# The S5 mixing stages of a four-layer trunk: fixed TensorE order, float32 in-projection in layer 0, u's round trip on the sync queue, decay tables ahead of the data

## The chip, the cores and the metric

The kernel runs on one core of a Trainium2 chip. The metric is the device time of one execution in microseconds (us), lower is better. The kernel before takes 1125.99 us, the median of three runs (1124.99 to 1126.99). A profile of one more execution shows what each engine did: TensorE (PE, and PEld for its weight loads), VectorE (DVE), ScalarE (ACT), GpSimd (POOL) and the sync engine (SP), which here only issues DMAs.

## What is computed

A trunk of four layers over 512 tokens of width 1024. Layers 0 and 3 mix with S5, layer 1 with HGRN2, layer 2 with sliding-window attention. Each layer adds `RMSNorm(branch(RMSNorm(h)))` to `h`. Only the S5 branch is touched by the change:

```python
def s5_branch(h, w_in, lam_re, lam_im, log_dt, b_re, b_im, c_re, c_im, d_skip, w_glu, b_glu, w_out):
    proj = h @ w_in                                   # 1024 -> 2048
    u, z = proj[..., :1024], proj[..., 1024:]
    uf = u.reshape(bsz, seq, 64, 16)                  # 64 groups of 16 channels
    ...                                               # a = exp(lambda dt), per group 64 complex states
    xr = jnp.einsum('blgh,gph->blgp', uf, bbr)
    xi = jnp.einsum('blgh,gph->blgp', uf, bbi)
    _, _, sr, si = lax.associative_scan(_complex_scan_combine, (a_r, a_i, xr, xi), axis=1)
    y = jnp.einsum('ghp,blgp->blgh', c_re, sr) - jnp.einsum('ghp,blgp->blgh', c_im, si)
    y = y.reshape(bsz, seq, 1024) + d_skip * u
    y = jax.nn.gelu(y)
    y = y * jax.nn.sigmoid(y @ w_glu + b_glu)
    return (y * jax.nn.silu(z)) @ w_out
```

## The kernel before

**Order of the work.** The program is written as straight code. A list scheduler decides the order of each engine's instructions from the code order and its own estimates; a buffer pool with a fixed number of buffers per tag decides what must wait for what. Once the order is fixed, each engine runs its instructions strictly in that order, and so do the two queues that issue DMAs, SP and ACT: a DMA that waits holds back everything behind it on its queue.

**Projections.** A float32 product is made of three matmuls in a reduced float32 format (fp32r): `whi·xh + whi·xl + wlo·xh`, for each of 8 slices k of the contraction, so 24 matmuls of 512 columns for one block of 128 outputs (`ws`, L146). ACT rounds a raw weight piece `wraw` to `whi` (L112), DVE subtracts to get `wlo` (L113); the normed input is split likewise into `xh` (ACT, L210) and `xl` (DVE, L211). The in-projection of an S5 layer has 16 blocks: 8 of u, 8 of z; it reads 16 weight pieces of 512 KB. The first 4 blocks are made in column pieces of 256 and 128 while the norm of the layer is still being computed (`first_blocks`).

**The S5 stage.** u's 8 blocks go through 8 rounds b = 0 to 7.
- `s5_tables`, once a layer: powers of the decay, tiles `ap`, `eb`, `ea`, many small DVE instructions; it stands behind the layer's norm statistics.
- `s5_rot`, once for two rounds: the scan's rotation table `rot` from `ea` and `eb` (DVE; products `rt` on POOL), copied by DMA to tile `rotf`.
- `s5_block_tables(b)`: parameters `prm` by DMA (one buffer), `q` (DVE, POOL `q12b`), the filter `vt = ap·q - ...` (DVE L483 and L485, POOL product `t` L484), its transposes and taps on PE (`kps`, `ktp`, `tps`, then `v` and `toep`), and `w` (DVE L514, POOL `t2w` L515, then L516 on DVE or, for odd b, on POOL).
- `s5_u(b)`: ACT copies the block to `ut`, a DMA writes it to DRAM (`ub`), another reads it back transposed as `u`; both are issued from the ACT queue.
- `s5_core(b)`: `xps = v·u` on PE (L537); ACT swaps halves (`xsw`); DVE rotates (`xa` L544, `xsw` L545, `xa` L546), scans (`r` L548); ACT swaps (`rsw` L550, L551); DVE rotates back (`r` L552, `rsw` L553, `spre` L555); PE makes `yps` from `toep·u` (L566) and `w·spre` (L568); ACT applies gelu (`ysb` L572). After each odd b, PE transposes two rounds of `ysb` (`ytp` L580) into `y`.

The gated output (`y @ w_glu`, written "glu" below) follows when all of `y` is there. The remaining 12 in-projection blocks are written in the code between the rounds and behind them, and the scheduler spreads their matmuls over the stage.

Of the kernel before, what the change touches and what calls it, by code (L numbers as in the profile page):

```python
# [9 lines left out]
F32 = mybir.dt.float32  # L10
# [6 lines left out]
P = 128  # L17
# [32 lines left out]
class Trunk:  # L50
# [30 lines left out]
    def w_load(self, i):  # L81
        if i >= len(self.wseq) or i in self.wraw or i in self.wcv:
            return
        name, j, c = self.wseq[i]
        shape, pieces = self.w_form(name)
        self.wraw[i] = []
        for v in range(pieces):
            raw = self.wpool.tile(shape, F32, tag="wraw", name="wraw", bufs=3)
            self.nc.sync.dma_start(out=raw, in_=self.a[name][j, c, v])
            self.wraw[i].append(raw)  # L90

    def w_conv(self, i):
        if i >= len(self.wseq) or i in self.wcv:
            return
# [7 lines left out]
        for raw in raws:  # L102
# [90 lines left out]
    def norm_xt(self, L, tbs):  # L193
# [7 lines left out]
        for k2 in range(KB // per):  # L201
# [5 lines left out]
            for kk in range(per):  # L207
# [3 lines left out]
                nc.vector.scalar_tensor_tensor(out=xl[:, k, c], in0=ps[:, kk, :], scalar=g, in1=xh[:, k, c].bitcast(F32), op0=ALU.mult, op1=ALU.subtract)  # L211
# [123 lines left out]
    def s5_tables(self, j):  # L335
# [73 lines left out]

        self.sp, self.tp, self.cp = [], [], []  # L410
# [13 lines left out]
    def s5_rot(self, pr):  # L424
# [23 lines left out]
        out = []  # L448
        for i in range(2):
            f = s.tile([P, 2, 512], F32, tag=f"rot{i}", name="rotf", bufs=1)  # L450
            src = rot[64 * i:64 * i + 64]
            nc.sync.dma_start(out=f[0:64], in_=src)
            nc.sync.dma_start(out=f[64:128], in_=src)
            out.append(f)
        return out

    def s5_open(self, L):

        self.tabcm = self.tc.tile_pool(name="tab", bufs=1, side="right", reuse_waits="tile")
        self.tab = self.tabcm.__enter__()  # L460
        self.s5_tables(L // 3)

    def s5_block_tables(self, j, b):
        nc, a, s = self.nc, self.a, self.scr
# [3 lines left out]
        nc.scalar.dma_start(out=prm, in_=a["s5_bc"][j, b])  # L468
# [26 lines left out]
        ktp = self.psum.tile([P, 2, 4, 32], F32, tag="ca", name="ktp", bufs=2)
        for i in range(2):
            nc.tensor.transpose(ktp[:, i].rearrange("p g h -> p (g h)"), kt[:, i, :], self.ident)
        dmx = self.tab.tile([P, 8, 16], F32, tag="dmx", name="dmx", bufs=1)
        nc.gpsimd.tensor_tensor(out=dmx, in0=bc(t["dm"][:, gs].unsqueeze(2), [P, 8, 16]), in1=bc(self.cst[:, CO_EYE16:CO_EYE16 + 16].unsqueeze(1), [P, 8, 16]), op=ALU.mult)
        ksb = self.tab.tile([P, 2, 4, 16], F32, tag="ksb", name="ksb", bufs=2)  # L500
        nc.vector.tensor_tensor(out=ksb, in0=ktp[:, :, :, 0:16], in1=dmx.rearrange("p (a g) h -> p a g h", a=2), op=ALU.add)
        toep = self.tp[b % 2]
        for jj in range(8):
            n = (jj + 1) * 16
            nc.sync.dma_start(out=toep[128 - n:128, jj, :, :], in_=ksb[0:n].rearrange("p a g h -> p (a g) h"))
        for hh in range(2):
# [3 lines left out]
            nc.scalar.activation(out=v[:, 4 * hh:4 * hh + 4, :], in_=tps, func=AF.Copy)  # L510

        w = s.tile(shp, F32, tag="w", name="w", bufs=2)
        t2 = self.tab.tile(shp, F32, tag="t2", name="t2w", bufs=1)
        nc.vector.tensor_tensor(out=w, in0=bc(t["ap"][:, 0, gs, 1:9].unsqueeze(3), shp), in1=bc(c1[:, :, 0:16].unsqueeze(2), shp), op=ALU.mult)  # L514
        nc.gpsimd.tensor_tensor(out=t2, in0=bc(t["ap"][:, 1, gs, 1:9].unsqueeze(3), shp), in1=bc(s2.unsqueeze(2), shp), op=ALU.mult)  # L515
        (nc.gpsimd if b % 2 else nc.vector).tensor_tensor(out=w, in0=w, in1=t2, op=ALU.subtract)  # L516
        return dict(v=v, w=w.rearrange("p g j h -> p g (j h)"), toep=toep, sp=self.sp[b % 2])

    def s5_u(self, b, ps):
# [5 lines left out]
        nc.scalar.dma_start(out=ub.rearrange("j f c -> f j c"), in_=ut)  # L525
# [684 lines left out]
```

## Time and profile before

| | |
|---|---|
| median of three runs | 1125.99 us (1124.99 to 1126.99) |
| the profiled execution, its own time | 1127.56 us |
| its span in the trace | 1125.8 us |
| mean granted TensorE clock over the span | 0.968 of full speed |
| PE busy | 1039.3 us, 92% |
| DVE busy | 783.4 us, 70% |
| ACT busy | 516.8 us, 46% |
| POOL busy | 233.2 us, 21% |
| layer 0's S5 stage, up to the dense glu matmuls | 0 to about 203 us |
| layer 3's S5 stage, up to the dense glu matmuls | about 834 to 1033 us |

The span is the trace's time from the first to the last instruction; 1.76 us of the execution's own time lie outside of it. The busy shares are means over four layers with different limits, so a stage is read from its own stretch, not from this table.

### The profile page before, as it was taken

The page shows a single profiled execution, that of the slowest core. Times are in us where ns is not written, and L with a number is a line of the kernel's source. Part 1 is how long each engine was busy: PE and PEld are TensorE (multiplying, and loading weights), DVE is VectorE, ACT ScalarE, POOL GpSimd, SP SyncE. Part 2 cuts the span into 40 slices and gives each one's busy share as a digit, 9 for nine tenths or more (in the row PEclk, how much of TensorE's full clock was granted, in tenths as well). Part 3 has the DMA queues.
Part 4 walks back from the last instruction along what each step waited for, and adds up shares of the span by engine and source line. Part 5 has one row for each costly group of instructions (what it writes and reads, how often), then busy time and mean ns, then how long its engine had stood idle before and what let it go on. Part 6 is the DMA issues. An engine that isn't in the chain of part 4 may idle for free.

```text
span 1125.8 us, 16828 instructions
## 1 busy us (share of the span) xinstructions
PE 1039.3 (92%) x6384; PEld 863.8 (77%) x6384; DVE 783.4 (70%) x1442; ACT 516.8 (46%) x939; POOL 233.2 (21%) x218
## 2 busy tenths in 40 slices
PE   5987898999999999999999989999998888778997
PEld 5866676878899898989888966666688676667885
DVE  6979998675566475656656455566569799995752
ACT  5444444754332324142344344888545254446540
POOL 2165553210200000000001121100011546550200
PEclk9989989999999999999999999999999899998999
DMA  7455425333130212222123443112134644434221
GB/s 244 136 143 141 102 86 128 131 120 114 53 111 22 94 39 83 69 75 76 36 79 102 108 116 100 38 53 80 57 128 126 168 107 139 115 91 140 95 91 56
DMA packets 60320, 112.32 MB, mean 100 GB/s; under 512 B 23632, under 2 KB 33488, under 8 KB 59856
## 3 DMA queue, kind: packets, MB, share of 16 engines
q1 hardware_dynamic: 34272, 87.58, 25.5%
q10 hardware_dynamic: 25968, 23.68, 7.2%
q8 instruction: 50, 0.82, 0.3%
q14 instruction: 30, 0.25, 0.1%
HBM read 87.11 MB, written 8.39 MB: 85 GB/s over the span
## 4 chain that ended last, share of the span: by engine, by line
PE 59%; DVE 23%; issue 6%; DMA 4%; ACT 4%; POOL 3%; ACTq 1%; DVEq 0%; SPq 0%; POOLq 0%
PE pj L146 22%; PE ops L160 14%; PE zps L160 4%; DVE wlo L113 4%; PE vps L160 4%; PE sps L711 2%; PE scps L909 2%; DVE vt L483 2%; PE aops L945 2%; DVE xsw L545 2%; DMA rsw<-rraw 1%; PE ptp L940 1%; DVE vt L485 1%; DMA rotf<-rot 1%; ACT whi L112 1%
## 5 line engine op out<-in xcount | busy, mean ns | idle before, releaser
L146 PE MATMUL pj<-xh,whi 128*128 128x512 f32 (+1 forms) x656 | 238.9, 367 | 0.9 <-ACT whi L112 0.9
L146 PE MATMUL pj<-xh,wlo 128*128 128x512 f32 (+1 forms) x656 | 239.5, 366 | 0.1
L146 PE MATMUL pj<-xl,whi 128*128 128x512 f32 (+1 forms) x656 | 237.9, 364 | 1.3 <-DVE xl L211 1.3
L113 DVE TENSOR_TENSOR wlo<-wraw,whi 128x1024 fp32r<-128x1024 f32 x132 | 172.4, 1311 | 74.5 <-ACT whi L112 67.6
L112 ACT ACTIVATE whi<-wraw 128x1024 fp32r<-128x1024 f32 x132 | 138.6, 1056 | 75.8 <-PE pj L146 31.8
L146 PEld LDWEIGHTS pj<-xh,wlo 128*128 128x128 f32 x656 | 129.0, 197 | 20.6 <-issue 6.1
L146 PEld LDWEIGHTS pj<-xh,whi 128*128 128x128 f32 x656 | 128.9, 198 | 20.5 <-issue 4.8
L146 PEld LDWEIGHTS pj<-xl,whi 128*128 128x128 f32 x656 | 129.0, 197 | 18.2 <-issue 2.7
L160 PE MATMUL ops<-whi,gh 128*128 128x512 f32 x256 | 101.8, 398 | 0.3 <-ACT gh L642 0.3
L160 PE MATMUL ops<-whi,gl 128*128 128x512 f32 x256 | 100.7, 394 | 0.0
L160 PE MATMUL ops<-wlo,gh 128*128 128x512 f32 x256 | 100.3, 392 | 0.0
L160 PEld LDWEIGHTS ops<-whi,gh 128*128 128x128 f32 x256 | 48.2, 188 | 11.3 <-ACT gh L642 1.1
L160 PEld LDWEIGHTS ops<-whi,gl 128*128 128x128 f32 x256 | 48.0, 188 | 11.2 <-DVE gl L643 0.9
L160 PEld LDWEIGHTS ops<-wlo,gh 128*128 128x128 f32 x256 | 48.2, 188 | 10.8 <-issue 1.1
L484 POOL TENSOR_TENSOR t<-ap,q 128x1024 f32<-128x1024 f32 x16 | 40.3, 2519 | 74.6 <-DVE q L475 37.5
L170 POOL TENSOR_SCALAR rs_m<-po_st 128x1 f32<-128x1 f32 x16 | 3.1, 191 | 252.5 <-DVE po_st L256 252.5
L146 PE MATMUL pj<-yh,whi 128*128 128x512 f32 x128 | 49.3, 399 | 4.2 <-ACT yh L621 4.2
L170 POOL TENSOR_SCALAR rs_m<-hss 128x4 f32<-128x4 f32 x8 | 1.6, 194 | 247.9 <-DVE hss L769 247.9
L210 ACT ACTIVATE xh<-xtp,gpre 128x128 fp32r<-128x128 f32 (+1 forms) x96 | 36.2, 400 | 32.8 <-DVE xl L211 20.9
L146 PE MATMUL pj<-yl,whi 128*128 128x512 f32 x128 | 50.1, 393 | 0.0
L146 PE MATMUL pj<-yh,wlo 128*128 128x512 f32 x128 | 50.1, 392 | 0.0
L252 DVE TENSOR_TENSOR yg<-ops,gpost 128x512 f32<-128x512 f32 x32 | 22.0, 689 | 40.0 <-ACT junk L250 39.6
(266 smaller groups left out, 2293.9 us busy)
## 6 DMA issues: line engine op xcount, KB each, us to landing
wraw<-in_s_in SPq DMA_DIRECT2D x32, 512.0 KB, 4.2
wraw<-in_hg_in SPq DMA_DIRECT2D x32, 512.0 KB, 3.5
wraw<-in_at_in SPq DMA_DIRECT2D x20, 512.0 KB, 4.2
rotf<-rot SPq DMA_DIRECT2D x32, 256.0 KB, 4.4
wraw<-in_s_glu SPq DMA_DIRECT2D x16, 512.0 KB, 3.7
wraw<-in_s_out SPq DMA_DIRECT2D x16, 512.0 KB, 3.5
prm<-in_s_bc ACTq DMA_DIRECT2D x16, 256.0 KB, 2.7
ub<-ut ACTq DMA_DIRECT2D x16, 256.0 KB, 3.2
```

The costliest lines, as they stand in the source:

```text
L112: nc.scalar.activation(out=hi, in_=raw, func=AF.Copy)
L113: nc.vector.tensor_tensor(out=lo, in0=raw, in1=hi.bitcast(F32), op=ALU.subtract)
L146: self.nc.tensor.matmul(ps, lhsT=l[k // 4][:, k % 4, c], rhs=r[:, k, n0:n1], start=k == 0 and n == 0, stop=k == KB - 1 and n == 2)
L160: self.nc.tensor.matmul(ps, lhsT=l[:, k, c], rhs=r[k // per][:, k % per, :], start=k == 0 and n == 0, stop=k == KB - 1 and n == 2)
L210: nc.scalar.activation(out=xh[:, k, c], in_=ps[:, kk, :], func=AF.Copy, scale=g)
L252: nc.vector.tensor_tensor(out=yg[:, tb, f], in0=ps, in1=gp[:, f], op=ALU.mult)
L483: nc.vector.tensor_tensor(out=vt, in0=bc(t["ap"][:, 0, gs, 0:8].unsqueeze(3), shp), in1=bc(q[:, 0].unsqueeze(2), shp), op=ALU.mult)
L484: nc.gpsimd.tensor_tensor(out=t2, in0=bc(t["ap"][:, 1, gs, 0:8].unsqueeze(3), shp), in1=bc(q[:, 1].unsqueeze(2), shp), op=ALU.mult)
L545: nc.vector.tensor_tensor(out=xsw, in0=xsw, in1=sin, op=ALU.mult)
L711: nc.tensor.matmul(ps[:, c, :], lhsT=k[:, c * 128:c * 128 + 128], rhs=q4[:, c, :, 1, :], start=True, stop=True)
L909: nc.tensor.matmul(ps[:, bb, lo:256], lhsT=self.q[r, 4 * p + 2 * b2 + bb, qs], rhs=self.k[r, p, ks], start=True, stop=True)
L945: nc.tensor.matmul(ops[64 * i:64 * i + 64].rearrange("p b q -> p (b q)"), lhsT=self.v[:, n - 1 + f, kv * 64:kv * 64 + 64], rhs=pts[i][:, f ...
```

## The change

It has six parts.
1. **Fixed PE order.** In both S5 layers the PE's instructions are taken out of the scheduler's hands and run in the order of the code. The in-projection's remaining 12 blocks become a generator of 96 steps (one k each), and `pump(n)` puts n steps between the pieces of the rounds. The other engines are scheduled as before.
2. **Plain float32 in layer 0's in-projection.** One float32 matmul for each k instead of three of fp32r. `whi`, `wlo` and `xl` are not made there; the raw weights are loaded into the buffers of `whi` and `wlo` (8 in all), so `wraw`'s three buffers are free for glu weights. Layer 3 keeps the three matmuls.
3. **u's trip from SP.** `ub` and `u` are issued from the SP queue.
4. **Tables ahead.** In layer 0 `s5_tables` no longer stands behind the norm statistics, and its memsets move to the program's start. In layer 3 it stays behind them.
5. **xps in halves.** Each of the 8 matmuls of `xps` becomes two of 64 output columns.
6. **Smaller functions.** `s5_block_tables` and `s5_core` are cut into `s5_v`, `s5_v_taps`, `s5_toep`, `s5_w`, `s5_states`, `s5_y` and `s5_yt`, so that they can be called one or two rounds ahead; `rotf` is copied for one round at a time.

```diff
+    def plain(self, i):
+        return i < len(self.wseq) and self.wseq[i][:2] == ("s5_in", 0) and self.layers[0] == 0
...
+            if self.plain(i):
+                raw = self.wpool.tile(shape, F32, tag=("whi", "wlo")[v], name="wraw", bufs=4)
+            else:
+                raw = self.wpool.tile(shape, F32, tag="wraw", name="wraw", bufs=3)
...
+        terms = ((hi, xh), (hi, xl), (lo, xh)) if lo is not None else ((hi, xh),)
         for k in range(KB):
-            for n, (l, r) in enumerate(((hi, xh), (hi, xl), (lo, xh))):
...
+            for n, (l, r) in enumerate(terms):
...
+            yield
...
-        nc.scalar.dma_start(out=ub.rearrange("j f c -> f j c"), in_=ut)
+        nc.sync.dma_start(out=ub.rearrange("j f c -> f j c"), in_=ut)
         u = s.tile([P, 8, 64], F32, tag="u", name="u", bufs=3)
-        nc.scalar.dma_start(out=u, in_=ub.rearrange("j (h g) c -> (j h) g c", g=8))
+        nc.sync.dma_start(out=u, in_=ub.rearrange("j (h g) c -> (j h) g c", g=8))
...
         for g in range(8):
-            nc.tensor.matmul(xps[:, g, :], lhsT=t["v"][:, g, :], rhs=u[:, g, :], start=True, stop=True)
+            for o in (0, 64):
+                nc.tensor.matmul(xps[o:o + 64, g, :], lhsT=d["v"][:, g, o:o + 64], rhs=u[:, g, :], start=True, stop=True)
...
+    def s5_rest(self):
+        nc = self.nc
+        for c in range(6):
+            w = self.w_next("s5_in")
+            for fb in range(2):
+                ps = self.pj()
+                yield from self.ws_steps(ps, w, fb, self.x, 0, T)
+                if c < 2:
+                    self.s5_u(4 + 2 * c + fb, ps)
+                else:
+                    nc.scalar.activation(out=self.z[:, 2 * (c - 2) + fb, :], in_=ps, func=AF.Copy)
...
-        with self.scratch("left"):
+        with self.scratch("left"), self.tc.manual_schedule(engines={mybir.EngineType.PE}):
             self.first_blocks(L, [lambda ps, b=b: self.s5_u(b, ps) for b in range(4)])
-            with self.behind(self.last_rstd, self.last_sq if L == 0 else None):
-                self.s5_open(L)
-                tabs = {0: self.s5_block_tables(j, 0)}
-            rot = self.s5_rot(0)
+            more = self.s5_rest()
...
+            with self.behind(self.last_rstd if L else None):
+                if L:
+                    self.s5_open()
+                self.s5_tables(j)
+                d = {0: self.s5_v(j, 0)}
+            self.s5_rot(0)
+            rot = {0: self.s5_rot_to(0), 1: self.s5_rot_to(1)}
+            self.s5_v_taps(0, d[0])
+            pump(3)
+            self.s5_toep(0, d[0])
+            self.s5_w(0, d[0])
+            d[1] = self.s5_v(j, 1)
+            pump(3)
             for b in range(8):
...
+                self.s5_states(b, d[b], rot.pop(b))
+                if b % 2 and b + 2 < 8:
+                    rot[b + 2] = self.s5_rot_to(b + 2)
+                pump(2)
                 if b + 1 < 8:
...
+                    self.s5_v_taps(b + 1, d[b + 1])
+                    pump(2)
+                    self.s5_toep(b + 1, d[b + 1])
+                    self.s5_w(b + 1, d[b + 1])
+                if b % 2 == 0 and b + 2 < 8:
+                    self.s5_rot(b // 2 + 1)
+                    rot[b + 2] = self.s5_rot_to(b + 2)
+                if b + 2 < 8:
+                    d[b + 2] = self.s5_v(j, b + 2)
+                pump(4)
+                self.s5_y(b, d.pop(b))
+                pump(3)
+                if b % 2:
+                    self.s5_yt(b // 2)
+            pump(96)
```

How this moves the instructions shows at three places. The first is PE around the first rounds of layer 0. Before, round 1's `xps` runs in two pieces among the in-projection's matmuls, which stand one by one in the order that the scheduler chose; `yps`'s half that needs round 0's `spre` (L568) comes 26 rows behind the first of these:

```order
L509 MATMUL tps<-cst,vt 128x128 x4
L537 MATMUL xps<-u,v 128x64 x4
L146 MATMUL pj<-xl,whi 128x512
L146 MATMUL pj<-xh,wlo 128x512
L146 MATMUL pj<-xh,whi 128x512
L537 MATMUL xps<-u,v 128x64 x4
```

After the change the same engine has round 0's `xps` as 16 smaller matmuls, eight in-projection steps and round 1's taps, then round 0's `yps`, and round 1's `xps` only three steps behind that:

```order
L578 MATMUL xps<-u,v 64x64 x16
L163 MATMUL pj<-xf,wraw 128x512 x2
L518 MATMUL kps<-vt,c_91 32x128 x8
L525 MATMUL tps<-cst,vt 128x128 x8
L163 MATMUL pj<-xf,wraw 128x512 x2
L535 MATMUL ktp<-cst,kt 128x128 x2
L163 MATMUL pj<-xf,wraw 128x512 x4
L610 MATMUL yps<-toep,u 64x128 x2
L612 MATMUL yps<-w,spre 64x128 x2
```

So round b+1's states now start behind round b's output, where before they could start ahead of it.

The second place is the SP queue at the program's start, where the rows are DMAs. Before, it reads the input and twelve weight pieces, and then the first round's `toep` and the `rotf` copies:

```order
L1079 DMA x_76<-in_x 128x1024 x4
L89 DMA wraw<-in_s_in 128x1024 x12
L505 DMA toep<-ksb 16x128
L505 DMA toep<-ksb 32x128
L505 DMA toep<-ksb 48x128
```

After, three pieces of glu weights stand early in it, and `ub` and `u` stand between and behind the `rotf` copies, which wait for `rot` on DVE:

```order
L1157 DMA x_93<-in_x 128x1024 x4
L93 DMA wraw<-in_s_in 128x1024 x8
L93 DMA wraw<-in_s_glu 128x1024 x3
L483 DMA rotf<-rot 64x1024
L564 DMA ub<-ut 128x8x64
L484 DMA rotf<-rot 64x1024
L483 DMA rotf<-rot 64x1024
L566 DMA u<-ub 128x512
```

So u's trip of round 0, which nothing held back on the ACT queue, now runs behind the first rotation table.

The third place is DVE between the ends of rounds 0 and 1 in layer 0. Before, a `wlo` stands in that stretch (two more follow before round 2's `xa`), and round 1's `xa` directly follows round 0's `spre`:

```order
L555 TENSOR_TENSOR spre<-r,rsw 128x8x63
L544 TENSOR_TENSOR xa<-xps,rotf 128x512
L545 TENSOR_TENSOR xsw<-xsw,rotf 128x512
L444 TENSOR_TENSOR rot<-ea,eb 128x512
L546 TENSOR_TENSOR xa<-xa,xsw 128x512
L501 TENSOR_TENSOR ksb<-ktp,dmx 128x128
L514 TENSOR_TENSOR w<-ap,c_602 128x1024
L548 SCALAR_TENSOR_TENSOR r<-mdec,xa 128x512
L516 TENSOR_TENSOR w<-w,t2w 128x1024
L473 TENSOR_TENSOR q_984<-prm,co 128x256
L113 TENSOR_TENSOR wlo<-wraw,whi 128x1024
```

After, there is no `wlo`, and round 2's tables (`vt`, `w`) stand between round 0's `spre` and round 1's `xa`:

```order
L595 TENSOR_TENSOR spre<-r,rsw 128x8x63
L508 TENSOR_TENSOR vt<-vt,t_638 128x1024
L553 TENSOR_TENSOR w<-ap,c_85 128x1024
L555 TENSOR_TENSOR w<-w,t2w 128x1024
L585 TENSOR_TENSOR xa<-xps,rotf 128x512
L586 TENSOR_TENSOR xsw<-xsw,rotf 128x512
L498 TENSOR_TENSOR q_765<-prm,co 128x256
L587 TENSOR_TENSOR xa<-xa,xsw 128x512
L589 SCALAR_TENSOR_TENSOR r<-mdec,xa 128x512
L593 TENSOR_TENSOR r<-r,rotf 128x512
L594 TENSOR_TENSOR rsw<-rsw,rotf 128x512
```

So table work fills the time in which PE turns `spre` into the next `xps`, and the scan and the rotation back follow each other with nothing between.

## Rows read from the trace of the kernel before

**Rows 1.** Busy time by stretch: us, count, busy of each engine, granted clock

```profile
core 0: us, PE busy (x) PEld busy (x) DVE busy (x) ACT busy (x) POOL busy (x), PEclk, DMA share, GB/s
15.00:52.00 37.00, 36.34 (x252) 34.18 (x253) 35.06 (x121) 20.11 (x41) 2.26 (x7) 1.00 0.54 163
86.00:198.00 112.00, 93.83 (x684) 74.29 (x685) 107.55 (x107) 55.25 (x88) 55.25 (x30) 0.92 0.42 113
834.00:910.00 76.00, 67.61 (x425) 59.06 (x424) 62.76 (x147) 32.75 (x63) 26.67 (x36) 0.91 0.46 126
911.00:1027.00 116.00, 93.59 (x684) 73.90 (x685) 106.14 (x106) 56.44 (x89) 54.91 (x30) 0.92 0.40 112
```

**Rows 2.** The chain that ended last, layer 0's rounds 0 and 6

```profile
86.29 0.67 DVE spre L555
...
173.37 4.22 DMA rotf<-rot
...
178.93 0.64 PE kps L492 x16
...
181.02 1.26 DVE xsw L545
182.30 2.75 DVE xa L546
...
187.04 0.64 ACT rsw L551
...
189.03 0.69 DVE spre L555
```

**Rows 3.** Timeline: first dense matmul, rounds 0 and 7 of layer 0, glu

```profile
15.30 0.58 PE L146 MATMUL pj<-xl,whi 128*128 128x256 f32 x1 [1.26 <-DVE xl L211]
62.86 1.89 PE L537 MATMUL xps<-u,v 128*128 128x64 f32 x16
197.40 1.20 PE L146 MATMUL pj<-yh,whi 128*128 128x512 f32 x4 [1.20 <-ACT yh L621]
197.98 0.68 DVE L555 TENSOR_TENSOR spre<-r,rsw 128x504 f32<-128x504 f32 x1
199.20 0.44 PE L568 MATMUL yps<-w,spre 128*64 128x128 f32 x4
200.56 0.39 PE L568 MATMUL yps<-w,spre 128*64 128x128 f32 x4
201.92 1.03 PE L580 MATMUL ytp<-cst,ysb 128*128 128x128 f32 x8
202.71 0.47 PE L146 MATMUL pj<-yh,wlo 128*128 128x512 f32 x1
```

**Rows 4.** Groups of instructions on DVE, 14.7 to 51.7 us: busy, mean ns

```profile
L113 DVE TENSOR_TENSOR wlo<-wraw,whi 128x1024 fp32r<-128x1024 f32 x8 | 9.9, 1232 | 0.5 <-ACT whi L112 0.5
L211 DVE SCALAR_TENSOR_TENSOR xl<-xtp,gpre,xh 128x128 fp32r<-128x128 f32 (+1 forms) x24 | 8.8, 390 | 0.7 <-ACT xh L210 0.7
```

**Rows 5.** The same view, 86 to 198 us

```profile
L113 DVE TENSOR_TENSOR wlo<-wraw,whi 128x1024 fp32r<-128x1024 f32 x9 | 14.8, 1647 | 0.2 <-ACT whi L112 0.2
```

**Rows 6.** Timeline of PE, fp32r steps (layer 3) and float32 matmuls (layer 2)

```profile
907.18 0.40 PE L146 MATMUL pj<-xl,whi 128*128 128x512 f32 x1
907.87 0.40 PE L146 MATMUL pj<-xl,whi 128*128 128x512 f32 x1
...
683.11 1.07 PE L945 MATMUL aops<-pt,av 128*64 128x512 f32 x2
...
802.84 2.69 PE L945 MATMUL aops<-pt,av 128*64 128x512 f32 x8
```

**Rows 7.** Timeline of DVE, rounds 0 and 7 of layer 3

```profile
910.85 0.67 DVE L555 TENSOR_TENSOR spre<-r,rsw 128x504 f32<-128x504 f32 x1
1027.19 0.68 DVE L555 TENSOR_TENSOR spre<-r,rsw 128x504 f32<-128x504 f32 x1
```

**Rows 8.** DMA issues, 0 to 203 us: KB each, median us to landing

```profile
rotf<-rot SPq DMA_DIRECT2D x16, 256.0 KB, 4.3
ub<-ut ACTq DMA_DIRECT2D x8, 256.0 KB, 3.2
```

More of the change, by code (lines that the diff above doesn't have):

```diff
@@ L110, in w_conv @@
                 lo = self.wpool.tile(shape, F32R, tag="wlo", name="wlo", bufs=4)
-            with self.behind(self.first_xs if i == 0 else None):
-                nc.scalar.activation(out=hi, in_=raw, func=AF.Copy)
-                nc.vector.tensor_tensor(out=lo, in0=raw, in1=hi.bitcast(F32), op=ALU.subtract)
+            nc.scalar.activation(out=hi, in_=raw, func=AF.Copy)
+            nc.vector.tensor_tensor(out=lo, in0=raw, in1=hi.bitcast(F32), op=ALU.subtract)
             his.append(hi)
@@ L137, in w_next, with ws, ws_steps @@
         return self.wcv.pop(i)
-    def ws(self, ps, w, fb, x, n0, n1):
+    def ws(self, *args):
+        for _ in self.ws_steps(*args):
+            pass
+    def ws_steps(self, ps, w, fb, x, n0, n1):
         hi, lo = w
@@ L447, in s5_rot, with s5_rot_to, s5_v @@
         nc.vector.tensor_tensor(out=rot[:, 1], in0=rot[:, 1], in1=rt[:, 1], op=ALU.add)
[L448 to L464, printed above, removed]
+        self.rots = rot
+    def s5_rot_to(self, b):
+        i = b % 2
+        f = self.scr.tile([P, 2, 512], F32, tag=f"rot{i}", name="rotf", bufs=1)
+        src = self.rots[64 * i:64 * i + 64]
+        self.nc.sync.dma_start(out=f[0:64], in_=src)
+        self.nc.sync.dma_start(out=f[64:128], in_=src)
+        return f
+    def s5_v(self, j, b):
+        nc = self.nc
         t = self.s5t
@@ L491, in s5_block_tables @@
             c = 32 * (g % 4)
-            nc.tensor.matmul(kps[c:c + 32, g // 4, :], lhsT=c1[:, g, :], rhs=vtf[:, g, :], start=True, stop=True)
+            nc.tensor.matmul(kps[c:c + 32, g // 4, :], lhsT=d["c1"][:, g, :], rhs=vtf[:, g, :], start=True, stop=True)
         kt = self.tab.tile([P, 2, 128], F32, tag="q12b", name="kt", bufs=1)
         nc.scalar.activation(out=kt, in_=kps, func=AF.Copy)
[L495 to L505, printed above, removed]
+        v = self.scr.tile([P, 8, 128], F32, tag="v", name="v", bufs=2)
         for hh in range(2):
@@ L608, in layer_s5 @@
-                self.s5_core(b, tabs.pop(b), rot[b % 2])
-            for c in range(4):
-                w = self.w_next("s5_in")
-                for fb in range(2):
-                    ps = self.pj()
-                    self.ws(ps, w, fb, self.x, 0, T)
-                    nc.scalar.activation(out=self.z[:, 2 * c + fb, :], in_=ps, func=AF.Copy)
+                    self.s5_v_taps(b + 1, d[b + 1])
+                    pump(2)
+                    self.s5_toep(b + 1, d[b + 1])
+                    self.s5_w(b + 1, d[b + 1])
@@ L1076, in run @@
             nc.scalar.dma_start(out=self.gpre, in_=a["norm_pre"])
+            if self.layers[0] == 0:
+                self.s5_open()
             x0 = self.act.tile([P, 4, D], F32, tag="y", name="x0")
```

108 lines of the change are left out of this document (67 added, 41 removed).

## The prediction

> **What bounds the kernel now.** I read the busy time by stretch first, because the page's shares mix four layers. Between rounds 0 and 7 of layer 0 DVE is busy 107.55 of 112 us, PE 93.83 and POOL 55.25; in layer 3 DVE has 106.14 of 116 [rows 1]. While the first blocks are made, PE has 36.34 of 37 and DVE 35.06. So both S5 stages are set by DVE, with PE close behind, and a granted TensorE clock of 0.91 or 0.92 there says that PE also pauses. Only these stages are touched (0 to 203 and 834 to 1033 us); the rest is taken as unchanged.
>
> Next comes the chain that ended last [rows 2]: inside a round it is a line of DVE instructions with ACT's swap between them, and it also waits 4.22 us for the copy of `rotf`. The milestones are the starts of `spre`: 86.29 and 197.98 in layer 0, 111.7 us for seven rounds [rows 2, 3]; 910.85 and 1027.19 in layer 3, 116.3 us [rows 7]. Dense glu work begins at 202.71 [rows 3]. Eleven of its matmuls had run earlier, the first four from 197.40 [rows 3]; at 0.23 us each (below) they are worth 2.5, so glu's effective start is 200.2, or 2.2 us behind the start of round 7's `spre`. I forecast when that point comes.
>
> **Plain float32: the gain.** Up to 52 us DVE is rid of 9.9 us of `wlo` and 8.8 of `xl` [rows 4], 18.7 together. From 86 to 198 us nine `wlo` cost 14.8 us [rows 5]; two or three of them are glu's, so some six go. The early ones took 1.23 us each, the late ones 1.65. At 1.23 six are worth 7.4 us, at 1.65 9.9; I take 8. The larger mean comes from waits at the port: `xa` too took 2.75 us in round 6, against 0.68 for the same size of `spre` [rows 2], and POOL is busy half of that stretch. By the Trainium skill ("Trainium Architecture — The Big Picture", "What this means for kernel authors") the port pair that DVE shares with GpSimd is an exclusive lock. By that rule a stall that goes with a `wlo` falls on the next DVE instruction, and the six would be worth 7.4 us, not 9.9; the 2.75 agrees with it.
>
> **Plain float32: the price on PE.** A step is now three matmuls, 907.18 to 907.87, 0.69 us [rows 6]. Float32 exists in layer 2 only: one product of 512 columns is an x2 row of 1.07 us, and four products in two halves of the array took 2.69, so 0.67 each [rows 6]. These are the bounds. A block of 128 outputs fills both halves, so the row of 1.07 is the nearer; an fp32r row of 0.40 starts every 0.23, so 0.17 of a row's length is overlap, and I take 0.90. For 128 steps (32 of the first blocks and 96 pumped) that is 115 us instead of 88, +27; the bounds give -3 and +49. The rule in the Trainium skill ("FP8 and Floating Point Precision", "TensorE Precision Notes") is four passes for true float32: four times 0.23, 0.92 a step, +29 us, and it speaks against the change; by the lower row the change would be free on PE.
>
> **The first round of layer 0.** From DVE's side round 0 comes 18.7 us earlier. From PE's side: dense work from 15.30 [rows 3], 32 steps of 0.90 to 44, the taps of round 0 and six steps (some 0.9, by `kps` with 0.64 [rows 2], and 5.4), and 1.4 us that I allow for ACT to copy the taps: `xps` at about 51.7, against 62.86 [rows 3], 11 earlier. Behind `xps`, `spre` took 23.4 us, with the second round's tables and one `wlo` on DVE between; if only the `wlo` (1.6) goes, `spre` is at 51.7 + 23.4 - 1.6 = 73.5. By DVE's side alone it is at 86.3 - 18.7 = 67.6, and some of the second round's tables can run while PE still makes the first blocks. I take 71.4, 15 us earlier, with 67.6 and 75.3 (the 11) as bounds.
>
> **Tables ahead.** The table's first rows stand on DVE ahead of `xs`, and I let the first `xs` come 2 to 3 us later. PE before became dense only at 15.30 [rows 3], held by `whi` and `xl`, which are gone; that covers the delay. Without this cover it costs up to 3 us.
>
> **u from SP.** The first `ub` stands behind a `rotf` copy that waits for `rot`, the last of the table work; that ended with DVE's dense stretch at 52 before [rows 1], so it ends 18.7 earlier, and with the first `vt` and `rot`'s own six instructions ahead of the copy I put it at 38 to 39. `ub` lands 3.2 us after issue [rows 8], and `u` is taken as the same: u(0) at about 45, hidden behind `xps` at 51.7. Cost 0. If `rot` were over 6 us later, `xps` would wait. Behind the waiting DMAs stand weight pieces and `toep`; a copy of 4.3 us [rows 8] that comes late is the bound, 0 to 4.3 us a round with a rotation table.
>
> **The fixed order: the period of a round.** Before, round b+1's `xps` could run ahead of round b's `yps`; now it comes three steps behind. This makes a closed loop: `spre` 0.7; `yps` 1.6 (199.20 to 200.56 and one piece [rows 3]); three steps 2.7; `xps`; two swaps on ACT 1.2 (0.64 each [rows 2]); then from `xsw` to `spre`, 181.02 to 189.03, 8.0 with its collision of 2.1 (2.75 less 0.68), so 5.9 to 8.0 [rows 2]. `xps` as 16 smaller instructions: 1.89 us was the whole before [rows 3]; half of that if two halves run side by side as the 2.69 row does, up to 1.89 if not; I take 1.0. Sum 13.1 to 15.2, and about 1 us for handing over: 14.1 to 16.2. DVE's own need is (107.55 - 8) / 7 = 14.2 a round [rows 1, 5]. Four rounds without new rotation work go at 14.5. In three, `rot`'s instructions and the next `vt` stand inside the loop, +2 to 3 us on 15.2 to 16.2: 18.2. Together 4 x 14.5 + 3 x 18.2 = 112.6.
>
> Round 7's `spre` starts at 71.4 + 112.6 = 184. Behind it: 0.7 + 1.6 + 2.7 (three steps) + 0.8 (`ytp`, 201.92 to 202.71 [rows 3]) + 3.6 (the last four steps) = 9.4. Glu from 193.4 against 200.2: **-6.8 us in layer 0**.
>
> **Layer 3.** DVE loses nothing there. Until round 0 it stood idle 13 of 76 us [rows 1], so the order can win 0 to 13 of it; nothing but the order works on that, and I take 3. A round needs 106.14 / 7 = 15.2 us of DVE, above the loop of its easy rounds; with 18 in three and 15.3 in four it is 115.2 against 116.3. The tail is 0.7 + 1.6 + 2.1 + 0.8 + 2.8 = 8.0 against 2.2, taken as in layer 0, +5.8. So -3 - 1.1 + 5.8 = **+1.7 us**, with -10 and +9 as bounds.
>
> Sum: -6.8 + 1.7 = -5.1. From the profiled 1127.56 this is 1122.5; it ran 1.57 above the median of 1125.99, so a median of **1121 us**.
>
> **Rivals.**
> - A, **the relief counts in full.** DVE rows fill the loop's gaps and PE becomes layer 0's bound: 115 us of steps and 42 for the rounds (5.3 each: `xps` 1.0, `yps` 1.6, taps and `ytp` put at 2.7 by `kps` and `ytp`) from 15.30 is 172, glu at some 175 to 180, -20 to -25; layer 3's tail is hidden by the earlier rounds, -3 to -5. About 1099. For it: 18.7 + 8 us leave an engine busy 96%. Against it: the loop has no slack at 14.5, and 115 at 1.07 would be 137.
> - B, **the loop is slower.** In fixed order every late tap (`kps` waits for `vt`) stops the steps behind it, and `spre` then waits on PE. At 18.5 a round in layer 0 and 17.3 in layer 3, glu is at 71.4 + 129.5 + 9.4 = 210.3, +10, and layer 3 has -3 + 4.8 + 5.8, +8: about 1144. It turns into a loss in layer 0 from 17.0 a round. For it: collisions of 2 us [rows 2] are no longer bridged by other rows, and one 4.2 us wait on `rotf` each two rounds is already there.
> - C, **nothing in sum.** The tail and the loop take back what the first round wins: 1126. For it: my periods are within 1 us of where it holds.
>
> **Chances.** Forecast, a gain of 3 to 15 us: 0.42. A, beyond 15: 0.18. B: 0.27. C, within 0.2%: 0.13; 0.2% is 2.25 us, about what a measurement of this kernel can tell from no change. So faster 0.6, same 0.13, slower 0.27. The range leaves out the outer half of A and of B: 1099 to 1139.
>
> **What would show it.** In layer 0 no `wlo` and no `xl`; float32 steps starting every 0.90 us; round 0's `spre` near 71 and round 7's near 184; glu's dense matmuls from 193 to 194. In layer 3 round 0's `spre` some 3 us earlier relative to the layer's start, and four steps alone on PE behind the last `ytp`. I am wrong if a step takes 1.07, if `xps` waits for u, or if the periods differ from 16.1 by more than 1 us, which is 7 us in each layer.

## The result and the profile after

The changed kernel takes **1180.62 us** (median of four runs, 1178.86 to 1182.24) against 1125.49 of the kernel before: 1.049 times, with a 95% interval of 1.0465 to 1.0515. So it is 55 us slower; forecast was 1121. The span of the profiled execution grew from 1125.8 to 1180.4 us.

The busy time by stretch of the changed kernel, from round 0's to round 7's `spre` in layer 0 and in layer 3, with the columns of [rows 1]:

```profile
core 0: us, PE busy (x) PEld busy (x) DVE busy (x) ACT busy (x) POOL busy (x), PEclk, DMA share, GB/s
83.00:216.00 133.00, 113.56 (x778) 62.67 (x778) 85.02 (x96) 50.36 (x83) 51.97 (x28) 0.90 0.37 96
941.00:1074.00 133.00, 103.67 (x853) 81.42 (x853) 102.07 (x105) 57.47 (x90) 49.23 (x29) 0.87 0.39 105
```

DVE, busy for 96% and 91% of these rounds before, now has 64% and 77%, and PE 85% and 78%. No engine fills the stages any more: they wait. The milestones stand in the timeline of the same kernel (single rows of it):

```profile
82.73 0.67 DVE L595 TENSOR_TENSOR spre<-r,rsw 128x504 f32<-128x504 f32 x1
216.35 0.68 DVE L595 TENSOR_TENSOR spre<-r,rsw 128x504 f32<-128x504 f32 x1
228.85 0.49 PE L163 MATMUL pj<-yh,whi 128*128 128x512 f32 x1 [1.21 <-ACT yh L697]
940.82 0.67 DVE L595 TENSOR_TENSOR spre<-r,rsw 128x504 f32<-128x504 f32 x1
1074.22 0.68 DVE L595 TENSOR_TENSOR spre<-r,rsw 128x504 f32<-128x504 f32 x1
1085.45 0.50 PE L163 MATMUL pj<-yh,whi 128*128 128x512 f32 x1 [1.21 <-ACT yh L697]
```

From these and [rows 3, 7] comes the account that the rest of this text explains. "Tail" is the time from round 7's `spre` to glu's start; of before it is taken less the glu matmuls that had run earlier, as in the prediction; layer 3's own is 3.2, where the prediction took layer 0's 2.2. Layer 3's way to round 0's `spre` is counted from the layer's first copy `ut` (862.3 and 891.7 us).

| us | before | after | difference | forecast |
|---|---|---|---|---|
| layer 0: round 0's `spre` | 86.3 | 82.7 | -3.6 | -14.9 |
| layer 0: seven rounds | 111.7 | 133.6 | +21.9 | +0.9 |
| layer 0: tail | 2.2 | 12.5 | +10.3 | +7.2 |
| layer 3: to round 0's `spre` | 48.6 | 49.1 | +0.5 | -3 |
| layer 3: seven rounds | 116.3 | 133.4 | +17.1 | -1.1 |
| layer 3: tail | 3.2 | 11.2 | +8.0 | +5.8 |

The rows add up to 54.2 of the 54.6 us by which the span grew.

**The loop of layer 0.** The chain that ended last in the changed kernel, round 2 to round 3 of layer 0 (start, length, what; the pieces between these are left out):

```profile
121.41 0.59 DVE spre L595
122.01 0.55 DVE q L500
122.63 2.98 POOL t L507
125.63 1.24 DVE vt L508
126.94 2.86 POOL t2w L554
129.82 5.52 DMA prm<-in_s_bc
135.36 0.41 ACT c L502
135.78 0.59 ACT xsw L581
136.39 0.60 ACT xsw L582
137.01 0.69 DVE xa L585
139.06 1.24 DVE r L589
142.29 0.68 DVE rsw L594
143.21 0.96 DVE spre L595
144.18 0.55 DVE q L500
144.80 2.98 POOL t L507
```

Read it as a circle. Round 4's table work (`q` and `vt` on DVE, `t` and `t2w` on POOL) stands behind round 2's `spre`. When `t2w` has read `prm`, the one buffer of `prm` is free and round 5's parameters are fetched. ACT's copy `c` waits for them, and ACT's swap `xsw` of round 3, whose `xps` PE had done by 129, stands behind `c`. Only then can round 3 rotate, scan and write its `spre`, and round 5's `q` follows. This turn and the next two took 21.8, 22.9 and 18.8 us from `spre` to `spre`. In the four turns from round 1 to round 5 `xsw` starts 22.5 us in sum behind the end of its `xps`. A second coupling lies close beside it: POOL's `q12b` of round 5 waited 13.23 us, until 143.02, for the buffer that it shares with `kt`. Rows of PE and POOL from the timeline:

```profile
127.83 1.15 PE L578 MATMUL xps<-u,v 128*64 128x64 f32 x32
143.02 0.62 POOL L499 TENSOR_TENSOR q12b<-prm,co 128x256 f32<-128x256 f32 x1 [13.23 <-PE ktp L535]
```

**The loop of layer 3.** The same view, round 2 to round 3 there:

```profile
983.34 0.60 DVE spre L595
983.99 0.69 PE yps L612 x4
...
987.24 3.40 PE pj L163 x9
990.64 1.08 PE xps L578 x32
...
994.30 0.69 DVE xa L585
...
1002.04 1.14 DVE vt L506
1003.18 0.60 DVE spre L595
```

This is the loop that the prediction closed, `spre`, `yps`, three steps, `xps` and back, but it takes 19.8 us, where 15.3 was forecast for a round without rotation work and 18 for one with it. The stretches of the same kernel around 984 us show one reason (columns as above):

```profile
978.00:983.90 5.90, 0.23 (x4) 0.00 (x0) 5.02 (x8) 3.31 (x5) 2.40 (x2) 0.91 0.17 40
983.99:987.10 3.11, 3.11 (x28) 2.85 (x28) 2.21 (x2) 0.00 (x0) 1.95 (x1) 0.50 0.50 106
987.20:989.40 2.20, 2.20 (x7) 1.80 (x6) 2.01 (x2) 0.60 (x1) 0.79 (x1) 0.50 0.66 188
989.50:991.00 1.50, 1.50 (x19) 1.06 (x19) 0.90 (x1) 0.00 (x0) 0.00 (x0) 0.95 0.94 208
```

PE stands still for 5.76 us in front of `yps`. When `spre` comes, the granted clock is 0.50, the 1.2 GHz level, until about 989.4: `yps` takes 3.25 us instead of 1.6 [rows 3], and nine rows of steps 3.40 instead of 2.1. In round 5, where PE waited 0.98 us, they took 1.75 and 2.34. So the waiting engine is also slow at the moment when the loop needs it: 2.6 us in this round, 0 to 2.6 in the others (`yps` took 3.1 to 3.3 us in six of the seven), some 12 us over the seven.

### The profile page after: what moved, and what is told of

It is laid out like the page before. It is cut to its first block, busy times and chain, and to the rows that moved or that the text cites. A ratio compares the mean times of both kernels' runs of the same rounds, so it can differ in the third digit from the quotient of the medians.

```text
span 1180.4 us, 16956 instructions
## 1 busy us (share of the span) xinstructions
PE 1055.7 (89%) x6480; PEld 838.4 (71%) x6480; DVE 730.9 (62%) x1402; ACT 500.7 (42%) x924; POOL 225.3 (19%) x218
## 4 chain that ended last, share of the span: by engine, by line
PE 61%; DVE 14%; ACT 4%; issue 4%; DMA 3%; POOL 3%; ACTq 1%; SPq 0%; DVEq 0%; POOLq 0%
PE pj L163 25%; PE ops L178 13%; PE zps L178 4%; PE vps L178 3%; PE sps L787 2%; PE scps L985 2%; PE aops L1021 2%; PE yps L612 2%; DMA prm<-in_s_bc 1%; DMA rsw<-rraw 1%; DVE wlo L124 1%; PE ptp L1016 1%; PE yps L610 1%; POOL t2w L554 1%; DVE r L589 1%
## 5 line engine op out<-in xcount | busy, mean ns | idle before, releaser
L124 DVE TENSOR_TENSOR wlo<-wraw,whi 128x1024 fp32r<-128x1024 f32 x116 | 146.4, 1268 | 98.4 <-ACT whi L123 80.0
L163 PE MATMUL pj<-xh,whi 128*128 128x512 f32 (+1 forms) x496 | 183.8, 371 | 0.0
L163 PE MATMUL pj<-xh,wlo 128*128 128x512 f32 (+1 forms) x496 | 177.8, 359 | 0.0
L163 PE MATMUL pj<-xl,whi 128*128 128x512 f32 (+1 forms) x496 | 177.2, 358 | 0.0
L163 PE MATMUL pj<-xf,wraw 128*128 128x512 f32 (+1 forms) x320 | 130.7, 556 | 0.0
L163 PEld LDWEIGHTS pj<-xh,whi 128*128 128x128 f32 x496 | 97.5, 197 | 16.6 <-issue 5.6
L163 PEld LDWEIGHTS pj<-xh,wlo 128*128 128x128 f32 x496 | 96.7, 195 | 14.3 <-issue 2.1
L163 PEld LDWEIGHTS pj<-xl,whi 128*128 128x128 f32 x496 | 97.4, 196 | 11.4 <-issue 1.0
L163 PEld LDWEIGHTS pj<-xf,wraw 128*128 128x128 f32 x320 | 63.0, 208 | 40.5 <-issue 36.2
L612 PE MATMUL yps<-w,spre 128*64 128x128 f32 x256 | 34.2, 352 | 43.2 <-DVE spre L595 43.2
L612 PEld LDWEIGHTS yps<-w,spre 128*64 128x64 f32 x256 | 21.9, 182 | 45.7 <-DVE spre L595 28.2
```

The lines of the kernel that those rows point to most:

```text
L612: nc.tensor.matmul(o, lhsT=sp[:, g, :], rhs=d["w"][:, g, :], start=False, stop=True)
```

## The experiments

Layers are read as in the table: rounds and tail of layer 0, then of layer 3.

### The order, the parameter buffer, and float32 inside the new order

The first run wrote the rounds in the order of before again and left PE to the scheduler; the other parts stayed:

```diff
-        with self.scratch("left"), self.tc.manual_schedule(engines={mybir.EngineType.PE}):
+        with self.scratch("left"):
...
             for b in range(8):
+                if b % 2 == 0 and b:
+                    self.s5_rot(b // 2)
+                    rot = {b: self.s5_rot_to(b), b + 1: self.s5_rot_to(b + 1)}
+                if b + 1 < 8:
+                    d[b + 1] = tables(b + 1)
...
                 self.s5_states(b, d[b], rot.pop(b))
...
                 self.s5_y(b, d.pop(b))
...
```

> The changed kernel with the rounds written in the order of before and PE's order left to the scheduler again; plain float32, u's trip on the sync queue, the tables ahead and xps in halves stay. Theory O (the hand-written order of the rounds costs the time, by a loop through one-buffer tiles): layer 3 comes back to about 116 us for its seven rounds and layer 0 to 112 or less, so 1126 or below. Theory P (float32 steps, the sync queue or the halves of xps cost it): 1150 or more, with seven rounds of about 130 us in layer 0.

1145.37 us, 1.0167 (1.0125 to 1.0208). Neither number: the old order gives back 35 us, and some 18 stay. The profile of this kernel is read further down.

The second gave `prm` two buffers. To make room, `lam`, `th`, `red_n`, `sin` and `cos` share tags with table tiles that are written later:

```diff
-        lam = s.tile([P, 3, N], F32, tag="lam", name="lam", bufs=1)
+        lam = s.tile([P, 3, N], F32, tag="prm", name="lam", bufs=2)
...
-        prm = self.tab.tile([P, 4, 128], F32, tag="prm", name="prm", bufs=1)
+        prm = self.tab.tile([P, 4, 128], F32, tag="prm", name="prm", bufs=2)
```

> The changed kernel with two buffers for prm (room made by letting short-lived table tiles share tags). Theory O1 (the loop goes from t2w through the parameter DMA to ACT's copy c, which stands ahead of the swap xsw on ACT): the DMA of 2.6 to 5.5 us leaves the loop, 3 us a round or more, so 20 us less in each S5 layer, about 1140. Theory O2 (the loop is that of the states alone: spre, yps, three steps, xps, and back): nothing, 1175 to 1185. Theory O3 (the loop closes through kt and q12b, which share one buffer): little, 1170 to 1180.

1158.11 us, 1.0286. Layer 0's rounds fell from 133.6 to 124.2 us and its round 0 came 7 us earlier (75.6); layer 3's rounds only from 133.4 to 131.2. So the loop through `prm` is real, it is mainly layer 0's, and its buffer is worth 22 us in all (4.5 of them ahead of layer 3's round 0). Theory O1's 20 us in each layer fell: in the four turns from round 1 to round 5 `xsw` now starts 4.5 us in sum behind `xps` instead of 22.5, but `xa` then starts 9.4 us in sum behind `xsw`, where it was 1.4, behind DVE's rows ahead of it, above all the rotation table `rot`.

The third also gave two buffers to the tag of `q12b` and `kt`:

```diff
-        q2 = self.tab.tile([P, 2, 8, 16], F32, tag="q12b", name="q12b", bufs=1)
+        q2 = self.tab.tile([P, 2, 8, 16], F32, tag="q12b", name="q12b", bufs=2)
...
-        kt = self.tab.tile([P, 2, 128], F32, tag="q12b", name="kt", bufs=1)
+        kt = self.tab.tile([P, 2, 128], F32, tag="q12b", name="kt", bufs=2)
```

> The changed kernel with two buffers for prm and two for the tag that q12b and kt share. Theory O1: as with prm alone, about 1140. Theory O2: 1175 to 1185. Theory O3 (q12b of the round after next waits for the transposes of kt, which the fixed order puts behind the states): clearly less than with prm alone, 1130 to 1140.

1180.97 us: worse than `prm` alone, with rounds of 133.9 and 144.5 us. Theory O3 fell as stated. With the buffer free, the scheduler's order puts `q` and both `vt` between `xa` and `spre`, inside the loop, in four of layer 0's seven rounds and in five of layer 3's. Rows of DVE in layer 3 of this run:

```profile
987.96 0.42 DVE L500 TENSOR_TENSOR q<-q,q12b 128x256 f32<-128x256 f32 x1
...
988.90 2.96 DVE L506 TENSOR_TENSOR vt<-ap,q 128x1024 f32<-128x1024 f32 x1
...
993.10 1.21 DVE L508 TENSOR_TENSOR vt<-vt,t 128x1024 f32<-128x1024 f32 x1
```

That is 4.6 us in such a round. With `prm` alone none of the three stands there in layer 0's rounds, and all three only in layer 3's first (`q` and one `vt` in its next three). So the order of DVE goes with the 23 us; that it alone makes them is not shown.

The fourth took plain float32 out of the changed kernel:

```diff
-        return i < len(self.wseq) and self.wseq[i][:2] == ("s5_in", 0) and self.layers[0] == 0
+        return False
```

> The changed kernel with layer 0's in-projection in three fp32r matmuls again. If PE's float32 steps carry layer 0's loss: about 10 to 20 us less, 1160 to 1170. If layer 0's loss is the same loop as layer 3's, which has no float32: the first round of layer 0 comes later by some 10 to 15 us and the rounds stay near 19 us, so 1185 to 1195.

1182.16 us: the same. Layer 0's rounds are 135.2 us without float32. Round 0's `spre` did not come 10 to 15 us later, as expected, but 3.6 earlier (79.1), and glu 2.2 earlier. Inside the new order the longer steps cost next to nothing, and DVE's relief brings nothing.

### The rounds' order in detail

Round b+1's `xps` ahead of round b's `yps`:

```diff
...
                 pump(4)
+                if b + 1 < 8:
+                    states(b + 1)
                 self.s5_y(b, d.pop(b))
```

> The changed kernel, still in a fixed PE order, with round b+1's xps placed ahead of round b's yps, right behind the four steps. Theory O2 (the loop spre, yps, three steps, xps and back to spre sets the period): round b+1 no longer waits for round b's output, so the seven rounds fall by 4 us and more each, to about 105 to 118 us in both layers, in sum near 1125. Theory O1 (prm's buffer and ACT's copy c): layer 0 keeps its 134 us, since c still stands ahead of xsw; in sum 1165 to 1180.

1179.97 us, no gain: layer 0's rounds 140.7, layer 3's 129.8. Theory O2's 105 to 118 fell in both layers. In layer 3, where this loop is on the chain, opening it brought only 3.6 us: PE then waits 20.9 us for `kt` in its rounds, against 0.75 in the changed kernel. So the loop of the states is not all that holds layer 3. The same with two buffers for `prm`:

> The changed kernel, still in a fixed PE order, with both: two buffers for prm, and round b+1's xps ahead of round b's yps. Alone the two gave 22 us and nothing. Theory M (two loops lie over each other, and taking one away leaves the other): together they give clearly more than 22, rounds of 15 to 16 us in both layers, 1125 to 1140. Theory N (the late taps in the fixed order are a third bound of the same size): as with prm alone, 1150 to 1165.

1168.83 us, 1.037: worse than `prm` alone, and outside the ranges of both theories. So theory M fell for this pair, and the late taps that theory N names show in the timeline of this run, layer 3:

```profile
963.87 0.63 ACT L591 ACTIVATE rsw<-r 64x512 f32<-64x512 f32 x1 [3.69 <-DVE r L589]
...
965.68 0.37 ACT L520 ACTIVATE kt<-kps 128x256 f32<-128x256 f32 x1
...
966.11 1.11 PE L525 MATMUL tps<-cst,vt 128*128 128x128 f32 x4 [4.76 <-ACT kt L520]
```

`kt` was ready to be copied at 960, but it stands on ACT behind round b+1's `rsw`, which waits for the scan; in PE's fixed order the steps stand behind `tps`, so PE waits 4.76 us. In this stretch (920 to 1075 us) PE waits 21.9 us for `kt`, in six waits.

All seven steps ahead of `yps`, with two buffers for `prm`:

```diff
-                pump(4)
+                pump(7)
                 self.s5_y(b, d.pop(b))
-                pump(3)
```

> The changed kernel with two buffers for prm and all seven steps ahead of yps instead of four ahead and three behind. Theory M: the loop spre, yps, three steps, xps loses its steps (2.0 us in layer 3, 2.6 in layer 0, more at the low clock), and the wait ahead of yps is filled: 2 to 3 us a round in both layers, 1115 to 1130. Theory N: the wait ahead of yps only changes its place, 1150 to 1160.

1139.95 us, 1.0114: 18 us less than with `prm` alone. Rounds 121.2 and 123.6, tails 9.0 and 8.3 instead of 10.9 and 11.3. The clock is one visible part, in the timeline of PE in rounds 2 and 3 of layer 3:

```profile
953.08 0.69 PE L612 MATMUL yps<-w,spre 128*64 128x128 f32 x4 [4.92 <-DVE spre L595]
953.56 0.64 PE L610 MATMUL yps<-toep,u 128*64 128x128 f32 x4
...
971.06 0.44 PE L612 MATMUL yps<-w,spre 128*64 128x128 f32 x4 [1.05 <-DVE spre L595]
971.30 0.42 PE L610 MATMUL yps<-toep,u 128*64 128x128 f32 x4
```

In round 3 the wait is 1.05 us, against 3.32 in the same round of the changed kernel; groups of four start some 0.23 us apart, not 0.43 as at 984 us, and `yps` takes 1.75 us. In rounds 2 and 4 the wait is still 4.92 and 3.98 and `yps` 3.25. So `yps` is slow in two of the seven rounds, not in six. The direction is theory M's, the size is not: 3 us less in layer 0's rounds and 8 in layer 3's, where 14 to 21 were expected, and 2 and 3 in the tails.

Without plain float32 on top of that (`plain` returns `False`, as above):

> The run with two buffers for prm and all seven steps ahead of yps, without plain float32. If float32's longer steps were hidden by the loop in the fixed order: glu of layer 0 starts within 3 us of that run or later, since DVE's work comes back, 1138 to 1150. If PE was the bound there: 5 to 15 us less, 1125 to 1135.

1142.92 us; glu of layer 0 starts at 210.4 instead of 204.1, and nearly all of that is there at round 0's `spre` (79.8 against 73.9). So in an order that waits less plain float32 is worth 6 us there, as the first alternative said; of the whole time only 3 us show, and the intervals of the two runs overlap.

### Each part alone, on the kernel before

First the order: the changed kernel's rounds and its fixed PE order, written in its smaller functions, and nothing else of it.

```diff
-        with self.scratch("left"):
+        with self.scratch("left"), self.tc.manual_schedule(engines={mybir.EngineType.PE}):
...
             with self.behind(self.last_rstd, self.last_sq if L == 0 else None):
...
+                self.s5_open()
+                self.s5_tables(j)
+                d = {0: self.s5_v(j, 0)}
...
+                pump(4)
+                self.s5_y(b, d.pop(b))
+                pump(3)
```

> The kernel before with the fixed PE order and the new order of the rounds alone: three fp32r matmuls, u from ACT, xps whole, tables behind the norm. If the order is the cause by itself: 1165 to 1185, with rounds near 19 us in both layers. If it needs the sync queue or the other parts: 1126 to 1150.

1186.47 us, 1.0547 (1.0506 to 1.0587), with rounds of 133.5 and 133.2 us and tails of 11.2 and 10.9. Three fp32r matmuls, u from ACT, `xps` whole and the tables behind the norm are as before in it. **The order carries the whole loss by itself**, in both layers; with the other parts the changed kernel is some 6 us below it, and the intervals of the two overlap. Both this run and the first change the order in which the rounds are written and PE's fixed order together; no run tells the two apart.

Then plain float32, with the raw weights in the buffers of `whi` and `wlo` as in the change:

```diff
...
-            for n, (l, r) in enumerate(((hi, xh), (hi, xl), (lo, xh))):
...
+            for n, (l, r) in enumerate(terms):
...
```

> The kernel before with plain float32 in layer 0 alone. If the relief of DVE counts (rival A of the prediction): 15 to 25 us less, 1100 to 1110. If PE's longer steps take it back: 1120 to 1130. If PE becomes the bound with waits of its own: up to 1145, and the loss of the run with the old rounds is explained by it.

1141.70 us, 1.0137 (1.0114 to 1.016). The seven rounds of layer 0 are faster, 105.8 us, and round 7's `spre` is at 192.2 instead of 198.0. But PE has 24 steps left. The timeline of PE in this run:

```profile
195.91 1.04 PE L595 MATMUL ytp<-cst,ysb 128*128 128x128 f32 x8
196.79 20.77 PE L157 MATMUL pj<-xf,wraw 128*128 128x512 f32 x48
218.76 0.50 PE L157 MATMUL pj<-yh,whi 128*128 128x512 f32 x1 [1.21 <-ACT yh L636]
```

Two rows make one step, so 24 steps in 20.6 us, 0.86 each. While they run DVE is busy for 1.23 of 20.70 us, and glu starts 18.6 us later than before.

The first experiment's kernel (all parts but the order) again, for its profile:

> The changed kernel with the rounds and PE's order of before once more, for its profile. If the order of the rounds is the cause in layer 3: its rounds take 110 to 117 us and its tail about 3. If plain float32 makes PE layer 0's bound: its last steps run alone on PE for 15 to 20 us behind the last transposes, and glu starts some 16 to 22 us later than before. In sum about 1145.

1144.84 us, and as expected: layer 3's rounds 112.5 us and its tail 3.7; in layer 0 rounds of 105.3, then the same 48 rows from 197.99 for 20.77 us, and glu at 220.0.

u's trip from the sync queue:

```diff
-        nc.scalar.dma_start(out=ub.rearrange("j f c -> f j c"), in_=ut)
+        nc.sync.dma_start(out=ub.rearrange("j f c -> f j c"), in_=ut)
...
-        nc.scalar.dma_start(out=u, in_=ub.rearrange("j (h g) c -> (j h) g c", g=8))
+        nc.sync.dma_start(out=u, in_=ub.rearrange("j (h g) c -> (j h) g c", g=8))
```

> The kernel before with u's trip issued from the sync queue alone. If ub and u are held behind rotf and weight pieces that wait: 5 to 15 us more in the two S5 layers together, and u lands after its xps could start. If they stay hidden behind the rounds: within 2 us of before.

1123.95 us, 0.9978 (0.9964 to 0.9993): it costs nothing, and is 3 us better.

`xps` in halves:

```diff
-            nc.tensor.matmul(xps[:, g, :], lhsT=t["v"][:, g, :], rhs=u[:, g, :], start=True, stop=True)
+            for o in (0, 64):
+                nc.tensor.matmul(xps[o:o + 64, g, :], lhsT=t["v"][:, g, o:o + 64], rhs=u[:, g, :], start=True, stop=True)
```

> The kernel before with xps in halves alone. If 16 smaller matmuls run side by side: xps takes about 1.1 us as in the changed kernel instead of 1.6 to 1.9, and the time is within 2 us of before or up to 5 us less. If the weight loads stay the limit: xps no shorter and the time the same.

1124.86 us, 0.9985 (0.9968 to 1.0001). A whole `xps` takes 1.15 us in this run, against 1.89 [rows 3], and the time shows nothing of it that can be told from no change.

The tables ahead in layer 0, with their memsets at the program's start:

```diff
...
-            with self.behind(self.last_rstd, self.last_sq if L == 0 else None):
-                self.s5_open(L)
+            with self.behind(self.last_rstd if L else None):
+                if L:
+                    self.s5_open(L)
+                self.s5_tables(j)
...
```

> The kernel before with the tables ahead of the data in layer 0 alone. The run with the old rounds was 4 us above plain float32 alone, with the other two parts worth -3 and -2: so the tables would cost some 5 to 9 us, by xs and the first blocks coming later on a DVE and PE that are both full there. If the cost came only from parts together: within 3 us of before.

1129.17 us, 1.0023 (1.0005 to 1.0042): about 2 us, less than supposed.

Two buffers for `prm` (the edit of above) on the kernel before with u from the sync queue:

> The kernel before with u's trip from the sync queue and two buffers for prm. If the wait for prm's buffer also held rounds before: 5 to 15 us less than before, 1110 to 1120. If DVE's 96 per cent was the bound and the wait was hidden: as with the sync queue alone, 1122 to 1126.

1125.93 us, 0.9995 (0.9979 to 1.0011). In the order of before the one buffer of `prm` costs nothing. It became a loop only with the new order.

u from the sync queue and `xps` in halves together (the two edits of above):

> The kernel before with the two parts that cost nothing alone, u from the sync queue and xps in halves. If their small gains add up: 1121 to 1123, clear of before. If they were no more than the scatter of the scheduler's orders: within 2 us of before.

**1121.74 us** against 1125.35, 0.9968 (0.9951 to 0.9986): u from the sync queue and `xps` in halves on the kernel before are 0.3% faster than the kernel before, and so faster than the changed kernel too.

## Why the prediction was wrong, step by step

- **What bounds the stage.** For before no run speaks against it: with plain float32 alone, which takes layer 0's `wlo` off DVE, its rounds fell from 111.7 to 105.8 us. But the prediction went on to use DVE's need of 14.2 us as what a round costs when its work fits. After the change the order, not a sum of work, sets the period: DVE is busy 64% and 77%.
- **The period of a round: the step that failed.** Forecast 16.1 us in layer 0 and 16.5 in layer 3, measured 19.1 in both (133.6 / 7 and 133.4 / 7): 39 of the 55 us. In layer 3 the loop that the prediction added up is on the chain, and its terms were too short: `yps` 3.25 for 1.6 and three steps 3.4 for 2.1, both at the granted clock of 0.50 behind PE's own wait; `vt` of 1.14 us on DVE between `rsw` and `spre` in an easy round too; and `ytp`, 0.8 us between the steps and the next `xps` behind each odd round, stood in the tail but not in the loop. That this loop alone sets the period is not shown: opened, the rounds fell by only 3.6 us. In layer 0 a second loop ruled that had no term at all, through `t2w`, `prm`'s buffer and ACT's `c`. Two buffers shortened its rounds by 9 us; seven steps ahead of `yps` took 3 from layer 0's rounds and 8 from layer 3's.
- **Rival B** named the mechanism's family, a slower loop, at 18.5 and 17.3 us, and gave 1144. It took the late taps for the cause. In the changed kernel PE waits for `kt` 11.0 us in layer 0's rounds and 0.75 in layer 3's; they become a bound only with `xps` first (21.9 us). So they are a third coupling, not the first.
- **Round 0 of layer 0.** Forecast 71.4, measured 82.7. The tables did end early: `rot` starts at 33.6 instead of 51.7. But the first blocks ended at 48.4, not 44 (I left out the transposes of `x` that stand among them, some 4 us), and then PE waited for `kt`. `kt` stood on ACT behind `c`, which waited 11.66 us for the second `prm`, and behind two copies `ut`, of which the second waited 2.86 us for `ut`'s one buffer. Rows of PE and ACT from the timeline of the changed kernel:

```profile
31.08 17.43 PE L163 MATMUL pj<-xf,wraw 128*128 128x256 f32 x80
48.44 0.65 PE L518 MATMUL kps<-vt,c 128*32 128x128 f32 x16
50.45 0.40 ACT L502 ACTIVATE c<-prm,cst 128x128 f32<-128x128 f32 x1 [11.66 <-DMA prm<-in_s_bc]
50.76 0.58 ACT L562 ACTIVATE ut<-pj 128x512 f32<-128x512 f32 x1
54.19 0.60 ACT L562 ACTIVATE ut<-pj 128x512 f32<-128x512 f32 x1 [2.86 <-DMA ub<-ut]
54.69 0.38 ACT L520 ACTIVATE kt<-kps 128x256 f32<-128x256 f32 x1
55.12 1.12 PE L525 MATMUL tps<-cst,vt 128*128 128x128 f32 x4 [5.44 <-ACT kt L520]
56.03 5.33 PE L163 MATMUL pj<-xf,wraw 128*128 128x512 f32 x6
64.08 1.15 PE L578 MATMUL xps<-u,v 128*64 128x64 f32 x32
```

  I had allowed 1.4 us for this copy. Behind the wait of 5.44 us the granted clock was 0.50 from 55.1 to 61.1 us, and three steps took 5.33 us instead of 2.7. `xps` came at 64.08 instead of 51.7.
- **The price of a float32 step** was right: 0.86 us measured, 0.90 forecast. The Trainium skill ("FP8 and Floating Point Precision", "TensorE Precision Notes") has four passes for true float32, by which four times 0.23 is an estimate of 0.92; the trace is near it. What it does to the time was not: alone it makes PE layer 0's bound and costs 15 us, and in the new order it is hidden. **Rival A** had this bound in it, but with 157 us of PE work. In the run with float32 alone PE is busy 177 of the 202 us from 15.3 to 217.5, so the gain of 20 to 25 became a loss.
- **The tails.** Forecast 9.4 and 8.0, measured 12.5 and 11.2; the sign and the reason were right (no glu matmul runs ahead any more), the half clock in front of them was missing (`yps` 2.29 and 3.25 us for 1.6), and so was PE's wait of 1.21 us for `yh` ahead of glu.
- **u from SP, tables ahead**: forecast 0; alone they measured -3 and +2 us. `xps` in halves was put at 1.0 us and took 1.15; alone its -1 us cannot be told from no change.

What stays open: how much of the loss the fixed order of PE makes and how much the order in which the rounds are written, what sets layer 3's period once the loop of the states is open, and what holds layer 0's remaining 121 us (seven steps ahead). There PE is busy 109 us and waits only 5.9 for `kt`.

## What to carry to other kernels

Here a new order of the rounds, fixed on one engine, turned the queues of two others (ACT, DVE) and a tile with one buffer into parts of a loop. Before writing such an order, follow each tile with one buffer through a whole round, with the issue of its DMA and whatever stands behind that wait on the same queue, and add the turn up; the busy shares say nothing about it. Put the work that can run at any time in front of an engine's wait, not behind it, and count what follows the wait at the clock that the trace shows there. When work is moved from a busy engine to another, count the second engine's whole sum against the stage's length first: with 128 steps of 0.86 us TensorE had 177 us of work, and became the bound.

## What the runs showed of the hardware

- In layer 3 of the changed kernel the granted TensorE clock stood at 0.50, the 1.2 GHz level, for some 5.4 us (984 to 989.4) behind a wait of 5.76 us, and `yps` took 3.25 us. With the steps moved ahead of it, the clock stood at 1.00 (970 to 973) behind a wait of 1.05 us, and `yps` took 1.75. In the same run, behind a wait of 4.92 us, it was 0.50 and 3.25 again.
- `xps` as 16 matmuls of 64 columns took 1.15 us instead of 1.89 [rows 3], both at a granted clock of 1.00, with twice the rows (x32 for x16). In the changed kernel the two halves of a pair start 0.01 us apart (64.08 us), though the weight loads doubled in number.
